# First conv unit of a hybrid decoder layer: one column chunk taken before its norm, two normalised meanwhile

## The chip, the cores and the metric

One core of one Trainium2 chip runs one layer of a decoder in float32. The metric is the device time in microseconds of the whole program. Engines: PE (TensorE, products), with PEld its weight loads; DVE (VectorE); ACT (ScalarE); POOL (GpSimd); SP, which only issues DMAs.

## The reference, cut to what matters

```
h = x * rsqrt(mean(x*x, over the 1024 channels) + eps) * g       # RMSNorm of 1040 positions
proj = h @ w_in                                                  # split among all branches
a, gate = u_conv                                                 # the conv branch's 2 x 1024 columns
y = a * sigmoid(gate)                                            # then a causal depthwise conv of 31 taps, ...
```

The other columns of proj are index queries and keys, attention q, k, v and merge gates; top-k attention, a merge product and a feed-forward part follow. rsqrt(mean) is one number for each position (a column here), so that it may be multiplied in before or after the product with w_in.

## The kernel before, in words

Channels lie on partitions, 8 tiles of 128 (k = 0 to 7); positions lie along the free dimension, 1044 with padding, cut into three chunks of 348 columns (c = 0, 1, 2). Every float32 product is made of three products of rounded parts: a value is split into a high part (a cast to fp32r) and a low part (value minus high part), and `mm` (L166 to L174, the matmul on L173) runs weight high x rows high, weight high x rows low, weight low x rows high, over the 8 tiles: 24 matmuls for one weight tile and one chunk.

`wload` (L114 to L127) loads a weight tile of 512 KB by SP (L117), casts its high part on ACT (L121) and makes the low part either on DVE (L123) or by an ACT negation (L125) and an accumulating DMA issued by POOL (L126). There are 2 raw buffers, 3 for high and 2 for low parts.

The start of the kernel: SP issues the first weight, x in 24 transfers (chunk by chunk, 8 tiles each, L210) with the second weight after the fourth of them (L212). WARM matmuls of the identity run on PE meanwhile (L222). Then, for each chunk in turn (L259 to L283): squares of the 8 tiles, six on ACT (L270) and two on DVE (L268); sums over partitions on PE, where a square is the stationary operand and a column of ones moves past it (L274: 3 blocks of 116 columns x 8 tiles, each recorded as 2 matmuls, so 48 records); the inverse root with one Newton step on [116, 3] tiles (`rstd_small`, L237 to L242: ACT's Sqrt is L238, the rest DVE); a broadcast over partitions by PE (L247, 6 records) into a PSUM bank; then per tile x times gain times that (L281, DVE), the cast to the high part `hh` (L282, ACT) and the low part `hl` (L283, DVE or POOL). The small sums and broadcasts use banks 6 and 7 in turn.

The first conv unit follows (L622 to L642): for each chunk 24 matmuls with the gate's weight into one bank triple and 24 with the value's into another; then tanh of half the gate on ACT (L631), (tanh + 1) times value on DVE (L641) into `g`, and the 31 taps of the depthwise conv (`conv_taps`, most of them on DVE, L554), which are dealt out as background work among the next units. Next come the index keys (L353, 72 matmuls, into the bank triple of the gate, so after the tanh has read it), four index-query units, merge gates, and conv units with other projections between them.

The order on each engine is fixed when the program is built: a planner takes instructions by priority and by its estimate of when their inputs are there (`urgent` raises the priority), and each engine then works its list in that order, waiting at semaphores. `tc.add_manual_dep` with NoSync is an order for the planner between two instructions of one engine, with no wait on the chip. Tiles of a full row of columns come from a pool of 31 (`ft`) or 4 (`tmp`) buffers.

## Time and profile before

| | us |
|---|---|
| median of 3 runs | 1860.74 (1859.44 to 1862.48) |
| profiled execution, its own time | 1865.77 |
| its span, first to last instruction | 1863.7 |
| busy: PE, DVE, ACT, POOL | 1790.6, 1231.9, 1049.3, 300.4 |
| mean granted PE clock | 0.975 of full speed |

The span is that of one profiled execution. Busy time of PE is from the start of a matmul to its modelled end, at whatever clock was granted: a busy PE at clock 0.5 does half the work. A row "[idle before <-releaser]" says how long the engine had waited and whose work ended the wait.

### The profile page before, as it was taken

The page shows a single profiled execution, that of the slowest core. Times are in us where ns is not written, and L with a number is a line of the kernel's source. Part 1 is how long each engine was busy: PE and PEld are TensorE (multiplying, and loading weights), DVE is VectorE, ACT ScalarE, POOL GpSimd, SP SyncE. Part 2 cuts the span into 40 slices and gives each one's busy share as a digit, 9 for nine tenths or more (in the row PEclk, how much of TensorE's full clock was granted, in tenths as well). Part 3 has the DMA queues.
Part 4 walks back from the last instruction along what each step waited for, and adds up shares of the span by engine and source line. Part 5 has one row for each costly group of instructions (what it writes and reads, how often), then busy time and mean ns, then how long its engine had stood idle before and what let it go on. Part 6 is the DMA issues. An engine that isn't in the chain of part 4 may idle for free. (4 is left out here: it accounts for less than half of the span.)

```text
span 1863.7 us, 29939 instructions
## 1 busy us (share of the span) xinstructions
PE 1790.6 (96%) x11956; PEld 1719.0 (92%) x11956; DVE 1231.9 (66%) x1949; ACT 1049.3 (56%) x1728; POOL 300.4 (16%) x310
## 2 busy tenths in 40 slices
PE   8989999999999999999999999899999999999987
PEld 7978899999999899899899999888999999999977
DVE  3598588997953472487843467845756575567677
ACT  3565587888999733488832246445434453444334
POOL 0243221111113122121100002011101100110002
PEclk7899999999999999999999999999999999999998
DMA  4434277776656488512246544365446634563432
GB/s 167 91 81 101 59 159 178 177 169 155 147 136 143 129 203 238 137 47 68 70 135 194 176 136 115 107 125 135 103 115 123 147 83 120 116 149 87 105 136 91
DMA packets 83899, 240.10 MB, mean 129 GB/s; under 512 B 8312, under 2 KB 28080, under 8 KB 83760
## 3 DMA queue, kind: packets, MB, share of 16 engines
q0 software_dynamic: 26208, 92.35, 27.9%
q1 hardware_dynamic: 57552, 145.84, 23.5%
q8 instruction: 93, 1.52, 0.3%
q14 instruction: 46, 0.38, 0.1%
HBM read 149.93 MB, written 65.09 MB: 115 GB/s over the span
## 5 line engine op out<-in xcount | busy, mean ns | idle before, releaser
L173 PE MATMUL PS<-hh,wh 128*128 128x342 f32 (+2 forms) x1096 | 196.0, 333 | 15.8 <-DVE qx0t L340 4.8
L1087 PE MATMUL PS<-B,ring 128*128 128x258 f32 (+1 forms) x1584 | 199.4, 286 | 5.5 <-DVE ub L1120 5.5
L1087 PEld LDWEIGHTS PS<-B,ring 128*128 128x128 f32 x1584 | 196.8, 193 | 8.2 <-DVE ub L1120 6.6
L173 PEld LDWEIGHTS PS<-hh,wh 128*128 128x128 f32 x1096 | 183.4, 195 | 20.2 <-DVE qx0t L340 5.2
L1155 PE MATMUL PS<-uh,ring 128*128 128x512 f32 (+2 forms) x736 | 188.6, 389 | 10.4 <-DVE x L1167 6.0
L459 ACT ACTIVATE junk<-sc,wn 128x1040 bf16<-128x1040 f32 (+6 forms) x217 | 182.3, 840 | 26.5 <-DVE wn L483 17.5
L173 PE MATMUL PS<-hh,wl 128*128 128x342 f32 (+2 forms) x1096 | 192.9, 328 | 0.8 <-DMA wl<-w_conv 0.8
L173 PE MATMUL PS<-hl,wh 128*128 128x342 f32 (+2 forms) x1096 | 191.1, 325 | 0.0
L1087 PE MATMUL PS<-h,ring 128*128 128x258 f32 (+1 forms) x1408 | 187.4, 282 | 3.7 <-ACT ring L1065 1.6
L173 PEld LDWEIGHTS PS<-hh,wl 128*128 128x128 f32 x1096 | 181.1, 192 | 2.7 <-DMA wl<-w_conv 1.1
L173 PEld LDWEIGHTS PS<-hl,wh 128*128 128x128 f32 x1096 | 179.4, 190 | 1.6
L1087 PEld LDWEIGHTS PS<-h,ring 128*128 128x128 f32 x1408 | 176.3, 189 | 4.4 <-ACT ring L1065 1.8
L1155 PEld LDWEIGHTS PS<-uh,ring 128*128 128x128 f32 x736 | 136.2, 190 | 39.7 <-issue 6.4
L121 ACT CAST wh<-wr 128x1024 fp32r<-128x1024 f32 x79 | 82.6, 1046 | 141.6 <-PE PS L173 69.5
L554 DVE SCALAR_TENSOR_TENSOR cb<-g,dwh,cb 128x1026 f32<-128x1026 f32 x105 | 138.0, 1316 | 34.8 <-DMA cb<-ct 34.7
L554 DVE SCALAR_TENSOR_TENSOR co<-g,dwh,co 128x1026 f32<-128x1026 f32 x113 | 152.2, 1350 | 1.4 <-ACT co L544 0.6
L1171 POOL DMA_DIRECT2D dx<-dn x72 | 62.4, 871 | 503.4 <-ACT dn L1170 498.0
L1065 ACT CAST ring<-ra 128x512 fp32r<-128x512 f32 x88 | 53.8, 620 | 126.3 <-PE PS L1087 64.6
L1066 DVE TENSOR_TENSOR ring<-ra,ring 128x512 fp32r<-128x512 f32 x88 | 60.0, 687 | 83.4 <-PE PS L1155 42.5
L1155 PE MATMUL PS<-ul,ring 128*128 128x512 f32 (+2 forms) x368 | 103.4, 390 | 0.0
L1087 PE MATMUL PS<-l,ring 128*128 128x258 f32 x704 | 100.1, 284 | 2.3 <-DMA l<-t 2.3
L1065 ACT CAST ring<-rb 128x512 fp32r<-128x512 f32 x66 | 41.0, 621 | 105.3 <-PE PS L1087 38.2
(438 smaller groups left out, 3552.8 us busy)
## 6 DMA issues: line engine op xcount, KB each, us to landing
dx<-dn POOLq DMA_DIRECT2D x72, 512.0 KB, 7.9
ra<-w_up SPq DMA_DIRECT2D x28, 512.0 KB, 3.8
rb<-w_up SPq DMA_DIRECT2D x22, 512.0 KB, 3.7
d<-w_down SPq DMA_DIRECT2D x22, 512.0 KB, 3.6
dth<-gt SPq DMA_DIRECT2D x16, 513.0 KB, 8.0
gate<-dth SPq DMA_DIRECT2D x16, 513.0 KB, 4.2
wr<-w_conv SPq DMA_DIRECT2D x16, 512.0 KB, 4.2
wr<-w_gate SPq DMA_DIRECT2D x16, 512.0 KB, 4.1
```

The lines of the kernel that those rows point to most:

```text
L121: act.copy(wh[:, :nk * P], raw[:, :nk * P])
L173: pe.matmul(ps[:, ci, :n], lhsT=ww[:, sl], rhs=rr[k][:, c0:c0 + n], start=(k == 0 and pi == 0), stop=(k == nk - 1 and pi == 2))
L459: act.activation(junk[:, :n], sc[j][:, PAD:PAD + n], AF.Sign, bias=bits.bitcast(F32)[:, slot[j]:slot[j] + 1], accum_out=cnt[:, slot[j]:slo ...
L554: dve.scalar_tensor_tensor(a, g[:, w:w + LQ], wt[w], a, op0=ALU.mult, op1=ALU.add)
L1065: hi = act.copy(t[:, w0], raw)
L1066: dve.tensor_tensor(t[:, w1], raw, f(t)[:, w0], op=ALU.subtract)
L1087: pe.matmul(ps[:, b, p0:p0 + nn], lhsT=t[:, o + k * P:o + (k + 1) * P], rhs=B[rows][k][e][:, r0:r0 + nn], start=(pi == 0 and k == 0), stop ...
L1155: pe.matmul(ps[:, c, :w], lhsT=t[:, wo:wo + P], rhs=rows[k][x][:, c0 + c * w:c0 + (c + 1) * w], start=(pi == 0 and k == 0), stop=(pi == 2 ...
L1171: pool.dma_start(d_x2[m], t[:, :SEQ], accum_op=ALU.add)
```

## The change

Seven things are altered, all in the start of the kernel, the first conv unit and the index keys.

1. Chunk 0 is taken raw: `raw_columns` makes `hh` and `hl` of x times gain, without 1/rms (ACT's scaled copy, DVE's scaled subtraction), and the first unit's 48 matmuls on chunk 0 use these. What comes out of them is multiplied by 1/rms afterwards: the gate's chunk 0 by a DVE multiply into `th` (the other two are copied there by ACT, and the tanh works on `th` in SBUF), the value's through one more DVE multiply on the first 348 columns of `g`.
2. Chunks are normalised in the order 1, 2, 0. 1/rms goes into an SBUF tile `rms` (ACT copy) instead of being read from PSUM. Chunk 0's rows are normalised last, for the index keys and everything behind them.
3. All 8 squares of a chunk are on ACT; those of tiles 4 to 7 are added to those of tiles 0 to 3 on DVE, so that PE sums four tiles and not eight (24 records a chunk).
4. Low parts: of chunks 1 and 0 all on DVE, after all the scalings of the chunk; of chunk 2 by an ACT negation and 8 accumulating DMAs that POOL issues. No subtraction is left on POOL.
5. In the first unit's chunks 1 and 2 and in the index keys the order of the three parts is high x high, weight low x rows high, weight high x rows low (`rows_last`); the index keys take the chunks in the order 1, 2, 0.
6. The second weight is loaded after all of chunk 0's x; the third weight's low part (the index keys') is made on DVE.
7. Orders for the planner (`behind`): chunk 1's squares after the raw casts; chunk 2's squares of tiles 0 to 3 after those, of tiles 4 to 7 after chunk 1's root; chunk 2's adds after chunk 1's Newton step; the next weight cast after chunk 2's rms copy.

```diff
@@ -86,6 +86,13 @@
     def f(t):
         return t.bitcast(F32)
 
+    def behind(a, b):
+
+        tc.add_manual_dep(a.ins, b.ins.name,
+                          mybir.DependencyInfo(mybir.DependencyClass.NoSync, mybir.DependencyReason.DATA), reason="order")
+
+    behind_act = [None]
+
     def urgent():
         return tc.high_priority(offset=600)
 
@@ -118,8 +125,11 @@
         wh = base.tile([P, KT * P], F32R, tag="wh", bufs=3, name=f"wh{i}")
         wl = base.tile([P, KT * P], F32R, tag="wl", bufs=2, name=f"wl{i}")
         with urgent():
-            act.copy(wh[:, :nk * P], raw[:, :nk * P])
-            if i < 2 or i >= ix_mg[0][0]:
+            e = act.copy(wh[:, :nk * P], raw[:, :nk * P])
+            if behind_act[0]:
+                behind(e, behind_act[0])
+                behind_act[0] = None
+            if i < 3 or i >= ix_mg[0][0]:
                 placed[0] = dve.tensor_tensor(wl[:, :nk * P], raw[:, :nk * P], f(wh)[:, :nk * P], op=ALU.subtract)
             else:
                 act.activation(wl[:, :nk * P], raw[:, :nk * P], AF.Copy, scale=-1.0)
@@ -163,10 +173,11 @@
     ix_mg = [[wadd(w_merge[m], KT) for m in range(KT)] for _ in range(2)]
     NPAIR = DFF // P
 
-    def mm(ps, w, rh, rl, nk, cols, woff=0):
+    def mm(ps, w, rh, rl, nk, cols, woff=0, rows_last=False):
 
         wh, wl = w
-        for pi, (ww, rr) in enumerate(((wh, rh), (wh, rl), (wl, rh))):
+        parts = ((wh, rh), (wl, rh), (wh, rl)) if rows_last else ((wh, rh), (wh, rl), (wl, rh))
+        for pi, (ww, rr) in enumerate(parts):
             for k in range(nk):
                 sl = slice(woff + k * P, woff + (k + 1) * P)
                 for ci, (c0, n) in enumerate(cols):
@@ -208,9 +219,8 @@
     for c in range(NCH):
         for k in range(KT):
             nc.sync.dma_start(xs[k][:, c * CW:(c + 1) * CW], xT[:, k, c * CW:(c + 1) * CW])
-            if c == 0 and k == KT // 2 - 1:
-                wload(1)
         if c == 0:
+            wload(1)
             nc.sync.dma_start(vec[:, V_DW:], vecs[:, V_DW:])
     ident = base.tile([P, P], F32, name="ident")
     make_identity(nc, ident)
@@ -229,23 +239,26 @@
         for b in range(nb):
             pe.matmul(dst[:w, b:b + 1], lhsT=src[:, c0 + b * w:c0 + (b + 1) * w], rhs=ones, start=True, stop=True)
 
+    root, newton = [None], [None]
+
     def rstd_small(src, w, n, name):
 
         v = base.tile([P, 9], F32, tag="stv", bufs=2, name=name + "v")[:w, :n]
         r = base.tile([P, 9], F32, tag="str", bufs=2, name=name + "r")[:w, :n]
         t = base.tile([P, 9], F32, tag="stt", bufs=2, name=name + "t")[:w, :n]
         dve.tensor_scalar(v, src[:w, :n], 1.0 / D, EPS, op0=ALU.mult, op1=ALU.add)
-        act.activation(t, v, AF.Sqrt)
+        root[0] = act.activation(t, v, AF.Sqrt)
         dve.reciprocal(r, t)
         dve.tensor_tensor(t, r, v, op=ALU.mult)
         dve.scalar_tensor_tensor(t, t, -0.5, r, op0=ALU.mult, op1=ALU.mult)
-        dve.scalar_tensor_tensor(r, t, 1.5, r, op0=ALU.add, op1=ALU.mult)
+        newton[0] = dve.scalar_tensor_tensor(r, t, 1.5, r, op0=ALU.add, op1=ALU.mult)
         return r
 
     def bcast_mm(dst, small, w, b0, nb):
         for b in range(nb):
             pe.matmul(dst[:, b * w:(b + 1) * w], lhsT=small[:, b0 + b:b0 + b + 1].to_broadcast([w, P]),
                       rhs=ident[:w, :w], start=True, stop=True)
+
 
 
     sc_pool = tc.tile_pool(name="sc", bufs=1)
@@ -255,32 +268,72 @@
     act.activation(warm, warm, AF.Sqrt)
     hh = [ft(f"hh{k}", F32R) for k in range(KT)]
     hl = [ft(f"hl{k}", F32R) for k in range(KT)]
+    rms = ft("rms")
     BW = CW // 3
-    for c in range(NCH):
+    first_ps = (psm(), psm())
+    tail, done = [None], [None]
+
+    def raw_columns(c):
+        cs = slice(c * CW, (c + 1) * CW)
+        for k in range(KT):
+            tail[0] = act.activation(hh[k][:, cs], xs[k][:, cs], AF.Copy, scale=vcol(V_MG + k))
+            dve.scalar_tensor_tensor(hl[k][:, cs], xs[k][:, cs], vcol(V_MG + k), f(hh[k])[:, cs], op0=ALU.mult,
+                                     op1=ALU.subtract)
+
+    def first_products(c):
+        for ps, w in zip(first_ps, units[0][2]):
+            mm(ps[:, c:c + 1, :], wdone[w], hh, hl, KT, LCOLS[c:c + 1], rows_last=c > 0)
+
+    def column_rms(c):
         cs = slice(c * CW, (c + 1) * CW)
         sqs = []
         for k in range(KT):
             if k % 3 == 0:
-                sqt = ft(f"sq{c}_{k}")
+                sqt = (tmp if c == 2 else ft)(f"sq{c}_{k}")
             sq = sqt[:, (k % 3) * CW:(k % 3 + 1) * CW]
             sqs.append(sq)
-            if k % 4 == 3:
-                dve.tensor_tensor(sq, xs[k][:, cs], xs[k][:, cs], op=ALU.mult)
-            else:
-                act.activation(sq, xs[k][:, cs], AF.Square)
+            e = act.activation(sq, xs[k][:, cs], AF.Square)
+            if c == 2 and k >= 4:
+                behind(e, root[0])
+            elif c:
+                behind(e, tail[0])
+                tail[0] = e
+            if k >= 4:
+                e = dve.tensor_tensor(sqs[k % 4], sqs[k % 4], sq, op=ALU.add)
+                if c == 2:
+                    behind(e, newton[0])
         sb = bank("s", (6, 7))
         for b in range(3):
-            for k in range(KT):
-                pe.matmul(sb[:BW, b:b + 1], lhsT=sqs[k][:, b * BW:(b + 1) * BW], rhs=ones, start=(k == 0),
-                          stop=(k == KT - 1))
+            for e in range(4):
+                pe.matmul(sb[:BW, b:b + 1], lhsT=sqs[e][:, b * BW:(b + 1) * BW], rhs=ones, start=(e == 0), stop=(e == 3))
         r = rstd_small(sb, BW, 3, f"n1{c}")
         sb = bank("s", (6, 7))
         bcast_mm(sb, r, BW, 0, 3)
+        done[0] = act.copy(rms[:, cs], sb[:, :CW])
+
+    def norm_columns(c):
+        cs = slice(c * CW, (c + 1) * CW)
         for k in range(KT):
             x = xs[k][:, cs]
-            dve.scalar_tensor_tensor(x, x, vcol(V_MG + k), sb[:, :CW], op0=ALU.mult, op1=ALU.mult)
+            dve.scalar_tensor_tensor(x, x, vcol(V_MG + k), rms[:, cs], op0=ALU.mult, op1=ALU.mult)
             act.copy(hh[k][:, cs], x)
-            (pool if k % 3 == 2 else dve).tensor_tensor(hl[k][:, cs], x, f(hh[k])[:, cs], op=ALU.subtract)
+        for k in range(KT):
+            if c == 2:
+                act.activation(hl[k][:, cs], f(hh[k])[:, cs], AF.Copy, scale=-1.0)
+                pool.dma_start(hl[k][:, cs], xs[k][:, cs], accum_op=ALU.add)
+            else:
+                dve.tensor_tensor(hl[k][:, cs], xs[k][:, cs], f(hh[k])[:, cs], op=ALU.subtract)
+
+    raw_columns(0)
+    first_products(0)
+    for c in (1, 2, 0):
+        with urgent():
+            column_rms(c)
+        norm_columns(c)
+        if c:
+            first_products(c)
+        if c == 2:
+            behind_act[0] = done[0]
     del xs
 
     def rope_table(name, src):
@@ -353,7 +406,8 @@
     def index_keys(w):
 
         ps = psm()
-        mm(ps, wget(w), hh, hl, KT, LCOLS)
+        for c in (1, 2, 0):
+            mm(ps[:, c:c + 1, :], wget(w), hh, hl, KT, LCOLS[c:c + 1], rows_last=True)
         kx, sw, wt = tmp("kxt"), tmp("kxs"), tmp("kxw")
         kh_, kl_ = kx_hl[:] = [ft("kxh", F32R), ft("kxl", F32R)]
         with urgent():
@@ -618,28 +672,32 @@
     GOFF = CONVW - 1 - Q0
     for kind, i, w in units:
         if kind == "conv":
-            ps = PS[:, 0:3, :] if i == 1 else psm()
+            if i:
+                ps = PS[:, 0:3, :] if i == 1 else psm()
+            th = tmp(f"th{i}")
             if i == 0:
-                wg, wa, psa = wget(w[0]), wget(w[1]), psm()
-                for c in range(NCH):
-                    mm(ps[:, c:c + 1, :], wg, hh, hl, KT, LCOLS[c:c + 1])
-                    mm(psa[:, c:c + 1, :], wa, hh, hl, KT, LCOLS[c:c + 1])
+                wget(w[1])
+                ps, pa = first_ps
+                with urgent():
+                    act.copy(c3(th[:, CW:LC], CW), ps[:, 1:, :CW])
+                    dve.tensor_tensor(th[:, :CW], ps[:, 0, :CW], rms[:, :CW], op=ALU.mult)
+                    act.activation(th[:, :LC], th[:, :LC], AF.Tanh, scale=0.5)
+                background(8, 1)
             else:
                 mm(ps, wget(w[0]), hh, hl, KT, LCOLS)
-            th = tmp(f"th{i}")
-            with urgent():
-                act.activation(c3(th[:, :LC], CW), ps[:, :, :CW], AF.Tanh, scale=0.5)
-            background(8, 1)
-            if i == 0:
-                ps = psa
-            else:
-                ps = PS[:, 0:3, :] if i == 1 else psm()
-                mm(ps, wget(w[1]), hh, hl, KT, LCOLS)
+                with urgent():
+                    act.activation(c3(th[:, :LC], CW), ps[:, :, :CW], AF.Tanh, scale=0.5)
+                background(8, 1)
+                pa = PS[:, 0:3, :] if i == 1 else psm()
+                mm(pa, wget(w[1]), hh, hl, KT, LCOLS)
             g = ft(f"g{i}")
             pool.memset(g[:, 0:GOFF], 0.0)
             with urgent():
-                dve.scalar_tensor_tensor(c3(g[:, GOFF:GOFF + LC], CW), c3(th[:, :LC], CW), 1.0, ps[:, :, :CW],
+                dve.scalar_tensor_tensor(c3(g[:, GOFF:GOFF + LC], CW), c3(th[:, :LC], CW), 1.0, pa[:, :, :CW],
                                          op0=ALU.add, op1=ALU.mult)
+                if i == 0:
+                    dve.tensor_tensor(g[:, GOFF:GOFF + CW], g[:, GOFF:GOFF + CW], rms[:, :CW], op=ALU.mult)
+                    del rms
             tasks.append(conv_taps(i, g))
             if i == KT - 1:
                 tasks.append(layer_norm())
@@ -1065,9 +1123,7 @@
             hi = act.copy(t[:, w0], raw)
             dve.tensor_tensor(t[:, w1], raw, f(t)[:, w0], op=ALU.subtract)
         if j < RB:
-            tc.add_manual_dep(hi.ins, placed[0].ins.name,
-                              mybir.DependencyInfo(mybir.DependencyClass.NoSync, mybir.DependencyReason.DATA),
-                              reason="room")
+            behind(hi, placed[0])
 
     def block(i, n):
 
```

## Rows read from the trace of the kernel before

**Rows 1.** Page, busy time, share of the span and instructions of each engine.
```profile
PE 1790.6 (96%) x11956; PEld 1719.0 (92%) x11956; DVE 1231.9 (66%) x1949; ACT 1049.3 (56%) x1728; POOL 300.4 (16%) x310
```

**Rows 2.** Busy time by stretch: from:to us, length, each engine, PE clock, DMA.
```profile
0.00:12.00 12.00, 8.59 (x56) 8.25 (x57) 3.51 (x5) 5.90 (x10) 2.41 (x31) 1.00 0.84 291
...
12.00:28.00 16.00, 10.42 (x47) 10.06 (x47) 9.00 (x20) 6.05 (x15) 1.89 (x2) 0.51 0.66 235
...
36.00:56.00 20.00, 20.00 (x91) 20.00 (x92) 8.71 (x24) 4.27 (x10) 1.97 (x3) 0.51 0.08 28
...
56.00:72.00 16.00, 14.05 (x88) 13.76 (x87) 7.08 (x14) 8.25 (x13) 2.92 (x3) 0.98 0.08 27
...
92.00:152.00 60.00, 51.08 (x244) 46.11 (x243) 59.81 (x52) 33.85 (x44) 26.14 (x14) 0.92 0.37 79
...
232.00:592.00 360.00, 356.78 (x2256) 355.52 (x2257) 291.78 (x407) 315.64 (x548) 66.65 (x72) 1.00 0.68 158
```

**Rows 3.** Timeline, 0 to 85 us: start, us taken, engine, line, operation, [idle before].
```profile
5.77 1.26 ACT L270 ACTIVATE sq<-x 128x348 f32<-128x348 f32 x3
...
16.47 0.16 DVE L237 TENSOR_SCALAR n10v<-PS 116x3 f32<-116x3 f32 x1 [5.35 <-PE PS L274]
...
17.72 1.63 PE L247 MATMUL PS<-ident,n10r 116*128 116x116 f32 x6 [1.29 <-DVE n10r L242]
...
22.16 1.04 ACT L121 CAST wh<-wr 128x1024 fp32r<-128x1024 f32 x1 [5.29 <-DMA wr<-w_idx]
...
23.64 4.72 PE L173 MATMUL PS<-hh,wh 128*128 128x348 f32 x15 [4.29 <-ACT hh L282]
...
26.18 4.71 ACT L270 ACTIVATE sq<-x 128x348 f32<-128x348 f32 x12
...
32.36 4.97 PE L274 MATMUL PS<-ones,sq 128*116 128x1 f32 x44
...
42.92 1.61 PE L247 MATMUL PS<-ident,n11r 116*128 116x116 f32 x6
...
44.32 7.37 PE L274 MATMUL PS<-ones,sq 128*116 128x1 f32 x38
...
44.56 3.99 DVE L281 SCALAR_TENSOR_TENSOR x<-x,vec,PS 128x348 f32<-128x348 f32 x8 [6.00 <-PE PS L247]
...
48.47 3.15 DVE L283 TENSOR_TENSOR hl<-x,hh 128x348 fp32r<-128x348 f32 x6
...
51.55 4.70 PE L173 MATMUL PS<-hh,wh 128*128 128x348 f32 x15
...
58.42 0.82 PE L247 MATMUL PS<-ident,n12r 116*128 116x116 f32 x6
...
72.12 4.08 PE L173 MATMUL PS<-hh,wh 128*128 128x348 f32 x24 [2.07 <-ACT th L631]
```

**Rows 4.** Groups of instructions by shape, 0 to 75 us: busy us, mean ns.
```profile
L274 PE MATMUL PS<-ones,sq 128*116 128x1 f32 x144 | 22.2, 283 | 1.9 <-ACT sq L270 1.7 <-DVE sq L268 0.2
...
L268 DVE TENSOR_TENSOR sq<-x 128x348 f32<-128x348 f32 x6 | 2.8, 510 | 0.0
...
L123 DVE TENSOR_TENSOR wl<-wr,wh 128x1024 fp32r<-128x1024 f32 x2 | 2.5, 1226 | 7.6 <-ACT wh L121 7.6
...
L631 ACT ACTIVATE th<-PS 128x1044 f32<-128x1044 f32 x1 | 1.0, 1041 | 0.0
```

**Rows 5.** Groups by shape on ACT, 1700 us to the end: a scaled copy.
```profile
L1211 ACT ACTIVATE x<-x,vec 128x256 f32<-128x256 f32 x8 | 3.9, 498 | 0.0
```

**Rows 6.** POOL's timeline near 1149 us: start, us taken, two DMA issues.
```profile
1149.17 1.75 POOL L982 DMA_DIRECT2D l<-t  x2 [0.69 <-ACT l L981]
```

**Rows 7.** Line L982's accumulating DMAs, 257 KB each, by source line.
```profile
DMA to landing us min/median/max: 3.4/5.2/6.8
```

**Rows 8.** PE's waits, 92 to 152 us: total, times, longest.
```profile
PE PS L173 <- DVE qx0t L340: 4.8, 1, 4.8
```

**Rows 9.** DVE's timeline, 92 to 152 us: one conv tap.
```profile
107.26 1.27 DVE L554 SCALAR_TENSOR_TENSOR co<-g,dwh,co 128x1026 f32<-128x1026 f32 x1
```

## The prediction

> **What bounds the kernel now.** I read the page's busy line first: PE is busy 96% of the span [rows 1], so the end moves only with PE's work, PE's clock, or PE's idle time. Then I took the busy time by stage [rows 2]. From 232 to 592 us PE is busy 356.8 of 360 us at clock 1.00: nothing to win or lose there except by a shift of the whole. The first 72 us are different. PE is busy in most of it, but the granted clock is 0.51 from 12 to 28 and from 36 to 56 us, half of full speed, that is 1.2 instead of 2.4 GHz. Last I read that stage in order of time [rows 3]. Its product work is one conv unit: 2 weights x 3 chunks x 24 = 144 products, which at the rate after 72 us (24 in 4.08, 0.17 us each) is 24.5 us. It takes until 70 us, because each chunk repeats one chain: squares, 48 one-column sums on PE, five small DVE steps and a root, six broadcasts, eight scalings on DVE, eight casts on ACT, and only then products. The first product starts at 23.64; the chunk-1 chain is through at 51.55, having waited in PE's own queue: its broadcast (42.92 us) and the 38 sums of chunk 2 (7.37 us) stand ahead of its products. At 72.12 the index keys begin. From there PE's work is the same before and after the change, so I forecast one number: when the index keys begin after it.
>
> **The change part by part.**
>
> *Chunk 0 raw.* Its products no longer wait for any statistic. They need x, which was squared from 5.77 us, and a scaled cast on ACT. One costs between 0.39 (twelve squares in 4.71) and 0.50 us (the scaled copies at the end, though of fewer elements) [rows 3, 5]; I take 0.45, since the width of the first and the scale of the second both apply: 8 x 0.45 from 5.9 to 9.5. The low parts on DVE, 8 x 0.53 (six in 3.15) after the weight's 1.23 [rows 3, 4], end near 11.5. The second weight now lies behind four more x transfers (0.7 MB, at the 291 GB/s of the first 12 us 2.4 us [rows 2]); its low part is ready near 13. That is covered by the 24 products of the first weight. The 48 products take 48 x 0.17 = 8.2 us at the high clock and 48 x 0.31 (15 in 4.70) = 15 at the low one, from about 7.5. They end between 16 and 23.
>
> *Chunk 1.* Squares 8 x 0.39 as x lands, to about 14.5; four DVE adds of 0.53, the last at 15.2; half the sums, 24 instead of 48, at 0.11 (44 in 4.97) or 0.19 (38 in 7.37): 2.7 or 4.6 us. Root and small steps 1.25 (16.47 to 17.72), broadcast 0.82 or 1.63, a copy to SBUF of 0.4, scaling (eight in 3.99) and cast 0.9 [rows 3]. First chunk-1 product at 21.5 to 24.5, as chunk 0's end: no gap worth counting. This is the large term: that point was 51.55. DVE then owes 4.0 of scaling, 4.2 of low parts and 2.1 of chunk 2's adds; the last low part comes near 33, the chunk's 48 products end near 34 (37 at the low clock).
>
> *Chunk 2.* Its rms is ready near 30, but DVE is free only near 33: scaling to 37, casts to 37.5, eight negations on ACT (0.39) to 40.6. Then POOL issues eight accumulating DMAs. The trace has no such transfer of 174 KB; the nearest are of 257 KB: two issues in 1.75, so 0.88 each, and 3.4 to 6.8 us to land, median 5.2 [rows 6, 7]. I take the median: last issue starts near 44.5, last low part near 50, the last products 0.5 later. The 32 products on the high parts are long done (39 to 43), so here PE waits for POOL's queue. Behind these eight on that queue stands only the third weight's transfer, needed 12 us into the index keys.
>
> *Halved sums* are inside the above: 72 of 144 records go, 72 x (22.2/144 = 0.154) = 11.1 us of PE [rows 4]; twelve DVE adds (6.4 us) come for six DVE squares (2.8) [rows 4].
>
> *After the unit.* Index keys reuse the gate's banks: ACT must copy two of them, 0.8 of the 1.04 that the tanh took [rows 4], so they begin near 51.5. If the clock dropped in PE's wait for chunk 2, their first 5 us run at half rate: 2.5 more. I take 54. Their third weight's low part comes from DVE (1.23) under the first 8 products; chunk 0's scaling and low parts, 8.2 us of DVE, lie under the 48 products on chunks 1 and 2 (8.2 us), and its squares earlier in ACT's gaps. The order put on the next cast (behind the rms copy) removes a stall like that of 22.16, where ACT sat 5.29 us for a weight's DMA with chunk 0's casts queued behind. Conv unit 0's g gains two DVE multiplies of 0.53 and its tanh now follows a copy: about 3 us later against the index keys. In 92 to 152 DVE is busy 59.8 of 60 and PE 51.1 [rows 2], so some of that comes back as PE waits: between 0 and 3 us, I take 0.5.
>
> *Sum.* 72.1 - 54 = 18 saved, less 0.5: 17.5. Ends: at the high clock, with landings in 3.4 us and the wait filled, the index keys start at 45 (27 saved); with the low clock throughout, 144 x 0.31 + 72 x 0.19 + 3 x 1.63 = 63 us from 7.5, so 70.5 (1.5 saved). The profiled run is 1865.77 (span 1863.7 and 2.1 around it); the sum gives 1848.3. The median shown, 1860.74, lies 5.0 under the profiled run: 1843.
>
> *The clock.* Rows first: from 36 to 56 us PE is busy 20.00 of 20 and the grant is 0.51; ahead of its fall at 36 PE ran one-column sums, and it is 0.98 over 56 to 72, after wide products from 51.55 [rows 2, 3]. The Trainium skill, page "TensorE: Matmul & The Clock Gate", Part 1, says that the engine is throttled by default and that being busy releases it. By that rule PE, fed from 7.5 on, would run high to the end of chunk 1 and the index keys would begin 2 to 3 us earlier than I take; by the rows a busy PE can stay low for 20 us. The rows decide, and the sum above leaves the chunk-0 clock open.
>
> **The rivals.**
> 1. *All works.* The clock stays at 1.00 and POOL's transfers land early. For it: sums halve and lie among wide products. Against it: the median landing is 5.2. Start 44 to 47: 25 to 28 saved, 1833 to 1836.
> 2. *DVE and POOL become the stage's bound.* DVE's work in it grows from about 30 to 38 us: raw low parts 4.2, adds 6.4, scalings 12, low parts 8.4, weights 3.7, small steps 3. If chunk 0's share runs ahead of chunk 2's scaling (8 us), or PE's queue holds the second weight's products behind low parts that land late and runs them at 0.31, the index keys start at 62 to 67: 5 to 10 saved, 1851 to 1856.
> 3. *Slower: conv taps get ahead.* PE's and DVE's orders are fixed beforehand from estimated times, and a new start gives a new order. DVE's taps of unit 0 take about 1.2 us each, and PE already waits 4.8 for one rope multiply behind them [rows 8, 9]. If the index-query multiplies each fall behind four or five more taps, four times, PE waits 16 to 24 us more. It decides from 15 more taps on (18 us): about 1866. Against it: taps and rope multiplies alternate nearly one to one, and nothing in that code is changed.
> 4. *No change.* The index keys do start early but chunk 0's normalised rows come so late (past 78 us) that their end stays. It would need 25 us of other DVE work ahead of them, which I don't find: 1858 to 1863.
>
> **How the numbers follow.** Forecast 1843 (1837 to 1849, 12 to 24 saved): 0.62. Rival 1: 0.13. Rival 2: 0.13. Rival 3: 0.07. Rival 4: 0.05. What can be told from no change here is 0.2%, 3.7 us. Faster by more: 0.62 + 0.13 + 0.13 = 0.88; within: 0.05; slower: 0.07. The range runs over rival 1's bound and rival 2's: 1832 to 1857, leaving out rivals 3 and 4 and a little below, some 0.15.
>
> **What would show it.** Right: a first wide product before 8 us; chunk 1's first between 21 and 25; one-column sums of 24 records per chunk; PE waiting for a DMA on the low parts near 40 to 50; index keys near 54; afterwards every stage shifted by the same. Wrong: clock 0.5 through the index keys; chunk 2's high parts behind chunk 0's scaling on DVE; the saving visible at the index keys but smaller at 232 us, which would be rival 3.

## The result, and the profile after

1843.91 us median (1840.62 to 1850.65, 6 runs) against 1861.58 for the kernel before in the same session. The ratio, taken over all runs and so not quite the quotient of the two medians, is 0.9912, 95% interval 0.9891 to 0.9933. The forecast was 1843. The execution that was profiled took 1850.64 us (span 1848.9), near the top of its runs; its span is 14.8 us under that of before.

Page, busy time, as [rows 1]: PE has 12 us less, the other three a little more.

```profile
PE 1778.6 (96%) x11884; PEld 1704.3 (92%) x11884; DVE 1239.5 (67%) x1964; ACT 1060.2 (57%) x1753; POOL 303.0 (16%) x311
```

Busy time by stretch, as [rows 2]. The clock of 36 to 56 us is 0.93 where it was 0.51. From 92 to 152 PE is busy even less than before, 49.94 of 60, and from 232 on it is as busy as it was (356.36 of 360, 356.78 before).

```profile
12.00:28.00 16.00, 14.71 (x88) 14.63 (x86) 8.11 (x20) 9.93 (x26) 0.11 (x1) 0.72 0.77 270
36.00:56.00 20.00, 18.73 (x115) 17.48 (x115) 13.46 (x30) 14.94 (x31) 8.11 (x9) 0.93 0.68 122
...
92.00:152.00 60.00, 49.94 (x258) 46.50 (x257) 55.61 (x56) 32.35 (x48) 22.56 (x14) 0.89 0.39 87
232.00:592.00 360.00, 356.36 (x2249) 354.93 (x2249) 289.58 (x402) 314.46 (x544) 72.12 (x72) 1.00 0.67 155
```

PE in order of time, as [rows 3], cut (L184 products, L308 one-column sums, L259 broadcasts): the raw products start at 6.99 and not at 23.64. Chunk 1's products (29.52) stand behind both its own sums and those of chunk 2. The index keys' first full run of products is at 53.13, not 72.12: 19.0 us earlier.

```profile
6.99 2.50 PE L184 MATMUL PS<-hh,wh 128*128 128x348 f32 x7
11.60 2.12 PE L184 MATMUL PS<-hh,wh 128*128 128x348 f32 x8 [2.12 <-ACT wh L128]
...
20.20 2.10 PE L308 MATMUL PS<-ones,sq 128*116 128x1 f32 x20
23.58 1.63 PE L259 MATMUL PS<-ident,n11r 116*128 116x116 f32 x6 [1.29 <-DVE n11r L254]
25.00 4.66 PE L308 MATMUL PS<-ones,sq 128*116 128x1 f32 x24
29.52 4.09 PE L184 MATMUL PS<-hh,wh 128*128 128x348 f32 x15
...
36.95 0.91 PE L259 MATMUL PS<-ident,n12r 116*128 116x116 f32 x6
...
51.88 0.58 PE L184 MATMUL PS<-hl,wh 128*128 128x348 f32 x2 [0.57 <-DMA hl<-x]
...
53.13 2.60 PE L184 MATMUL PS<-hh,wh 128*128 128x348 f32 x8 [0.36 <-ACT th L682]
```

ACT and then DVE behind the first unit: after PE's last product of it ACT copies two chunks of the gate (52.34), then serves a weight cast and two casts of rows, loads a table, and only at 56.10 comes the tanh. `g` is made at 57.21, 4.1 us after the index keys began (in the kernel before both were at 72.1). The first conv tap starts at 69.08, since it waits 9.76 us for a DMA. ACT, then DVE:

```profile
52.34 0.74 ACT L682 COPY th<-PS 128x696 f32<-128x696 f32 x1 [1.81 <-PE PS L184]
52.98 1.05 ACT L128 CAST wh<-wr 128x1024 fp32r<-128x1024 f32 x1
53.92 0.87 ACT L319 CAST hh<-x 128x348 fp32r<-128x348 f32 x2
54.81 1.28 ACT L684 ACT_TABLE_LOAD   x1
56.10 1.08 ACT L684 ACTIVATE th<-th 128x1044 f32<-128x1044 f32 x1
```

```profile
57.21 1.24 DVE L696 SCALAR_TENSOR_TENSOR g<-th,PS 128x1044 f32<-128x1044 f32 x1 [1.82 <-ACT th L684]
...
69.08 4.58 DVE L608 SCALAR_TENSOR_TENSOR cb<-g,dwh,cb 128x1026 f32<-128x1026 f32 x2 [9.76 <-DMA cb<-ct]
...
96.23 1.28 DVE L608 SCALAR_TENSOR_TENSOR co<-g,dwh,co 128x1026 f32<-128x1026 f32 x1
97.42 3.11 DVE L608 SCALAR_TENSOR_TENSOR cb<-g,dwh,cb 128x1026 f32<-128x1026 f32 x1
100.45 1.08 DVE L393 TENSOR_TENSOR qx1t<-PS,c 128x896 f32<-128x896 f32 x1
```

The same in the kernel before, ACT and DVE together; the first tap waited for that DMA there too, 10.64 us:

```profile
69.73 1.28 ACT L631 ACT_TABLE_LOAD   x1
71.03 1.04 ACT L631 ACTIVATE th<-PS 128x1044 f32<-128x1044 f32 x1
...
72.10 1.24 DVE L641 SCALAR_TENSOR_TENSOR g<-th,PS 128x1044 f32<-128x1044 f32 x1 [5.74 <-ACT th L631]
...
83.98 2.61 DVE L554 SCALAR_TENSOR_TENSOR cb<-g,dwh,cb 128x1026 f32<-128x1026 f32 x2 [10.64 <-DMA cb<-ct]
```

PE's waits from 92 to 240 us, as [rows 8]: the rope multiply of index query 1 stands behind a tap (97.42 above), and PE waits 5.9 us for it. The third row is new: a conv weight's low part, 2.4 us (0.8 in the kernel before).

```profile
PE PS L184 <- DVE qx1t L393: 5.9, 1, 5.9
PE PS L458 <- DVE r L467: 2.8, 1, 2.8
PE PS L184 <- DMA wl<-w_conv: 2.4, 1, 2.4
```

The tap at 97.42 takes 3.11 us, the one ahead of it 1.28. A multiply runs on POOL at that time:

```profile
97.17 2.27 POOL L447 TENSOR_TENSOR qs<-qx0t,qs 64x896 fp32r<-64x896 f32 x1 [4.15 <-ACT qs L446]
```

Of unit 0's 27 taps on DVE twenty take 1.27 to 1.29 us here, and the seven that take 2.15 to 3.26 all lie beside such an operation of POOL, 12 us more in all. POOL is the likely cause; no run took its operations away.

Landmarks tell where the 19 us went. The first merge gate's tanh came at 157.45 before and 138.34 after (19.1 earlier), the third one's at 309.36 and 294.12 (15.2 earlier), the last computing instruction 15.2 earlier. So 4 us were lost between the first and the third gate, and on balance none behind them. Before, then after:

```profile
157.45 1.01 ACT L665 ACTIVATE gt<-PS 128x1026 f32<-128x1026 f32 x1
...
309.36 1.00 ACT L665 ACTIVATE gt<-PS 128x1026 f32<-128x1026 f32 x1
```

```profile
138.34 1.01 ACT L723 ACTIVATE gt<-PS 128x1026 f32<-128x1026 f32 x1
...
294.12 1.00 ACT L723 ACTIVATE gt<-PS 128x1026 f32<-128x1026 f32 x1
```

### The profile page after: what moved, and what is told of

The parts are those of the page before. It is cut to its first block, busy times and chain, and to the rows that moved or that the text cites. A ratio compares the mean times of both kernels' runs of the same rounds, so it can differ in the third digit from the quotient of the medians.

```text
span 1848.9 us, 29862 instructions
## 1 busy us (share of the span) xinstructions
PE 1778.6 (96%) x11884; PEld 1704.3 (92%) x11884; DVE 1239.5 (67%) x1964; ACT 1060.2 (57%) x1753; POOL 303.0 (16%) x311
## 5 line engine op out<-in xcount | busy, mean ns | idle before, releaser
L184 PE MATMUL PS<-hh,wh 128*128 128x342 f32 (+2 forms) x1096 | 199.1, 333 | 14.7 <-DVE qx1t L393 5.9
L184 PEld LDWEIGHTS PS<-hh,wh 128*128 128x128 f32 x1096 | 183.6, 195 | 20.3 <-DVE qx1t L393 6.3
L184 PE MATMUL PS<-hh,wl 128*128 128x342 f32 (+2 forms) x1096 | 191.4, 326 | 2.4 <-DMA wl<-w_conv 2.4
L184 PE MATMUL PS<-hl,wh 128*128 128x342 f32 (+2 forms) x1096 | 192.6, 326 | 0.9 <-DMA hl<-x 0.9
L184 PEld LDWEIGHTS PS<-hh,wl 128*128 128x128 f32 x1096 | 179.9, 191 | 4.3 <-DMA wl<-w_conv 2.7
L184 PEld LDWEIGHTS PS<-hl,wh 128*128 128x128 f32 x1096 | 179.3, 190 | 3.3 <-DMA hl<-x 1.7
L608 DVE SCALAR_TENSOR_TENSOR cb<-g,dwh,cb 128x1026 f32<-128x1026 f32 x105 | 143.3, 1368 | 36.4 <-DMA cb<-ct 32.6
```

What stands on the lines that cost most here:

```text
L184: pe.matmul(ps[:, ci, :n], lhsT=ww[:, sl], rhs=rr[k][:, c0:c0 + n], start=(k == 0 and pi == 0), stop=(k == nk - 1 and pi == 2))
L608: dve.scalar_tensor_tensor(a, g[:, w:w + LQ], wt[w], a, op0=ALU.mult, op1=ALU.add)
```

## The experiments

Twelve kernels; each batch has its own runs of the kernel before (medians 1863.18 for experiments 1 to 4, 1860.85 for 5 to 8, 1864.93 for 9, 11 and 12, 1861.61 for 10). One table serves all. From the profiled execution, in us: "keys" is the index keys' first full run of products, "tap" the first DVE tap, "gate 1" and "gate 3" the tanh of those merge gates, "3-1" the time between them, "wait" PE's wait for a conv weight's low part in that time, "profiled" the execution's own time. "Median" and "ratio" (to the kernel before on the same chip, with its 95% interval) are over all runs. "Late shared taps" is the edit of experiment 5; "kernel 5" is the kernel of experiment 5.

```
   kernel                           keys   tap  gate 1 gate 3  3-1   wait profiled  median   ratio
   before                           72.1  84.0  157.5  309.4  151.9  0.8  1865.77
 2 halved sums alone                68.2  80.2  153.8  305.1  151.2  0.7  1862.08  1855.64  0.9963 (0.9951-0.9976)
 6 before, late shared taps         68.8  71.4  141.8  299.0  157.2  2.1  1850.27  1854.55  0.9962 (0.9947-0.9977)
 4 after, full sums                 64.4  77.1  145.2  302.6  157.4  3.7  1858.23  1855.69  0.9963 (0.9949-0.9976)
 3 after, no raw chunk              64.7  74.8  143.8  294.5  150.8  0.7  1849.35  1849.05  0.9936 (0.9914-0.9958)
 7  the same, late shared taps      62.1  65.1  137.6  293.6  156.0  2.1  1849.58  1852.34  0.9957 (0.9945-0.9969)
   after                            53.1  69.1  138.3  294.1  155.8  2.4  1850.64  1843.91  0.9912 (0.9891-0.9933)
 1 after again                      55.4  71.1  140.7  295.0  154.3  1.3  1850.96  1851.21  0.9933 (0.9910-0.9955)
 5 after, late shared taps          53.2  60.8  133.6  284.6  151.0  0.8  1841.85  1842.15  0.9907 (0.9894-0.9920)
11  the same, chunk 2 low on DVE    50.4  63.2  140.0  296.5  156.5  3.1  1855.15  1851.44  0.9931 (0.9915-0.9946)
12  the same, chunk 2's root first  58.4  66.1  139.0  289.7  150.7  0.7  1846.61  1847.53  0.9908 (0.9890-0.9926)
 8 after, weight 10's low on DVE    50.3  65.3  133.7  289.2  155.5  3.0  1850.46  1848.93  0.9942 (0.9929-0.9955)
 9 after, weight 11's low on DVE    54.3  69.0  137.6  294.0  156.5  2.9  1848.69  1852.68  0.9937 (0.9919-0.9956)
10 after, weight 12's low on DVE    50.9  65.6  134.2  285.5  151.3  none 1845.95  1845.68  0.9923 (0.9904-0.9943)
```

**1. The changed kernel again**, without an edit.

> The changed kernel once more, for a second profile. Mine (what is gained is gained before the index keys, all later differences are the order's): index keys begin at 53.1 +- 0.3 us again, and the 4.7 us that the first profile gives back between 174 and 230 us (a 2.4 us wait for a weight's low part at 201, then clock 0.64) are there again or, if the run is near 1842, smaller. Rival (the loss lies elsewhere, in the tail): the tanh of conv unit 1 stands at the same place in both profiles and the runs differ after 592 us. Time 1840 to 1851.

1851.21 (1841.65 to 1854.87). The two ratios, 0.9912 and 0.9933, have overlapping intervals, but one kernel spreads over 0.8%: a difference of 3 us between two kernels hardly shows in the totals.

The index keys began at 55.44, 2.3 us later and not within the 0.3 that was expected; the wait for the weight is there again, at 1.3 us. The order of work on every engine is the same in both executions, and up to 150 us also in kernels 8 to 10. So those five show what an execution does by itself: keys at 50.3 to 55.4, first tap at 65.3 to 71.1, gate 1 at 133.7 to 140.7. The time from the keys to gate 1 varies less, 83.3 to 85.3. One landmark against one other tells little under 5 us; a stretch between two landmarks tells more.

**2. The kernel before with halved sums, nothing else.**

```diff
+            if k >= 4:
+                dve.tensor_tensor(sqs[k % 4], sqs[k % 4], sq, op=ALU.add)
...
-            for k in range(KT):
+            for e in range(4):
...
```

> The kernel before with one part of the change: squares of tiles 4 to 7 added to those of 0 to 3 on DVE, PE sums four tiles. Mine: 72 records go from PE, but the chain through PE's queue stays; of 11 us some 5 to 9 are gained at the index keys (72.1 to 63 to 67), 1852 to 1856. Rival (the sums are the gain): 11 us or more, index keys at 61 or earlier, 1850 or less.

Ratio 0.9963, a total in the expected range. In the profiled execution, the slowest of its ten, the index keys come 4.0 us earlier, short of the 5 to 9 expected, and every later landmark by 3 to 4. These 4.0 do not stand clear of the spread: kernel 6, whose order is that of the kernel before up to its first tap, began its index keys 3.3 us earlier.

**3. The changed kernel, with all three chunks normalised (0, 1, 2), none raw.**

```diff
-    raw_columns(0)
-    first_products(0)
-    for c in (1, 2, 0):
+    for c in (0, 1, 2):
...
```

The rest of the edit goes with it: the tanh reads PSUM, nothing is multiplied by 1/rms afterwards, and the index keys take the chunks as 0, 1, 2.

> The changed kernel with chunk 0 normalised first like the others (order 0, 1, 2, tanh straight from PSUM, no multiply by 1/rms afterwards), everything else of the change kept. Mine: PE's first product moves from 7 to about 20 us and the index keys begin at 62 to 66, so 9 to 13 us of the gain go: 1852 to 1857. Rival (sums and orders are the gain, raw columns matter little because PE is not what ends the stage): index keys at 53 to 57, 1843 to 1848.

The index keys begin at 64.65, 11.5 us later than in the changed kernel, as expected. The total does not follow: 1849.05, under the 1852 to 1857 expected, and 0.9936 beside 0.9933 for the changed kernel in the same batch. The head start of 11.5 us is 5.7 at the first tap, 5.4 at the first gate, 0.4 at the third (5 us go between these gates, where this kernel waits 0.7 us for the weight and not 2.4; see experiment 10). DVE's timeline shows the first loss: here `g` follows the index keys' start at once, where the changed kernel needs 4.1 us more for its copy, table load and tanh; and here too the first tap waits 8.9 us for the DMA.

```profile
64.63 1.24 DVE L692 SCALAR_TENSOR_TENSOR g<-th,PS 128x1044 f32<-128x1044 f32 x1 [8.98 <-ACT th L680]
74.75 2.61 DVE L606 SCALAR_TENSOR_TENSOR cb<-g,dwh,cb 128x1026 f32<-128x1026 f32 x2 [8.87 <-DMA cb<-ct]
```

**4. The changed kernel, PE summing all eight tiles** (raw chunk kept).

```diff
-                e = dve.tensor_tensor(sqs[k % 4], sqs[k % 4], sq, op=ALU.add)
...
-            for e in range(4):
...
+            for k in range(KT):
...
```

> The changed kernel with PE summing all 8 squares again (48 records a chunk, no adds on DVE). Mine: chunk 1's sums stand before its products and cost 24 records more, 2.6 to 4.6 us, chunk 2's as much, partly hidden under the wait for POOL: index keys at 56 to 60, 1847 to 1852. Rival (the sums are the gain): 11 us back, index keys at 64, 1854 or more.

The index keys begin at 64.42, where the rival had them (64; 56 to 60 was expected): undoing the halved sums costs as much there as undoing the raw chunk, 11 us. The clock from 12 to 16 us is 0.57 in both executions compared, so that they start alike. The granted clock is 0.50 to 0.54 in six of the seven 4-us stretches from 24 to 52 us. The total is 1855.69 (0.9963), above the 1847 to 1852 expected.

After these four my theory was: once the index keys run, DVE and not PE sets the pace (it is busy 7.9 us or more of every 8 from 72 to 136 us), and its work begins with the first tap, so what counts is the first tap. The taps wait because two shared taps (made by ACT, added to both accumulators by DMAs) come first in the chain.

**5. The changed kernel, the shared taps of conv unit 0 issued after DVE's 27.**

```diff
+        if i:
+            shared_taps()
         for w in range(2, CONVW - shared):
...
+        if i == 0:
+            shared_taps()
```

> The changed kernel, with the two shared taps of conv unit 0 (made by ScalarE, added by a DMA) issued after VectorE's 27 taps instead of ahead of them, so that VectorE's first tap no longer waits 9.8 us for that DMA. Theory (from about 69 to 136 us VectorE is full with the taps and the rope multiplies, and the time follows its first tap, not the index keys' first product): index keys stay at 53 to 55, the first tap moves from 69.1 to about 61, TensorE's wait for the rope multiply of index query 1 (5.9 us) falls under 2, the first gate's tanh (138.3) comes 5 to 8 us earlier and the whole is 4 to 8 us under the changed kernel's 1844 to 1851, ratio to before 0.987 to 0.991. Rival (the time follows TensorE's order from the index keys on; VectorE only fills gaps): first tap at 61, the tanh within 1 us of 138, ratio 0.992 to 0.994 as for the changed kernel.

The first tap moves 8.3 us, with the index keys at 53.2 as in the changed kernel (clock from 12 to 16 us 0.58 and 0.57); the first gate comes 4.7 us earlier, just short of the 5 to 8 expected, and the third 9.5, of which 4.8 arise between the gates, where the wait for the weight is 0.8 us. From the keys to gate 1 it takes 80.4 us, outside the 83.3 to 85.3 of the five equal executions. 1842.15 (1841.36 to 1844.05): in the expected direction, though the interval overlaps both of the changed kernel's. The tap waits no longer for a DMA, but for ACT's first product:

```profile
60.77 1.29 DVE L611 SCALAR_TENSOR_TENSOR co<-g,dwh,co 128x1026 f32<-128x1026 f32 x1 [1.37 <-ACT co L598]
```

PE's waits from 92 to 240 us. The wait for index query 1 is halved, and query 2 has one of its own: 5.1 together, where 5.9 was expected to fall under 2.

```profile
PE PS L184 <- DVE qx1t L393: 2.7, 1, 2.7
PE PS L184 <- DVE qx2t L393: 2.4, 1, 2.4
...
PE PS L184 <- DMA wl<-w_conv: 0.8, 1, 0.8
```

**6. The same edit on the kernel before**, none of the change in it.

> The kernel before, with the same one edit of the shared taps and nothing of the change. Theory (VectorE's first tap sets it): index keys stay at 72.1, first tap moves from 84.0 to about 75, the first gate's tanh (157.5) 5 to 8 us earlier, total 1853 to 1857, ratio 0.995 to 0.997: the edit gives without any earlier products what the changed kernel only gets by 19 us of earlier products in part. Rival (TensorE's order from the index keys on sets it): within 1 us of before.

0.9962: 6 us, as expected. The index keys began 3.3 us earlier in this execution, which the edit does not touch; the first gate comes 15.6 us earlier, where 5 to 8 were expected. From 92 to 152 us PE's waits fall to these two rows, and its clock is 1.00 there instead of 0.92:

```profile
PE PS L173 <- DVE qx1t L340: 3.1, 1, 3.1
PE PS L173 <- ACT gt L670: 0.5, 1, 0.5
```

```profile
92.00:152.00 60.00, 56.31 (x307) 52.72 (x306) 52.23 (x50) 42.98 (x57) 30.43 (x19) 1.00 0.59 132
```

**7. No raw chunk (as 3), with the late shared taps.**

> Chunk 0 normalised first (as in the run before without raw products) together with the late shared taps. Theory (first tap sets it): first tap moves from 74.8 to about 67.5, total 3 to 7 us under the 1849 of the same kernel without the edit, ratio 0.990 to 0.992, and 3 to 7 us above the changed kernel with the late taps, since its gate came 7 us later: with the DMA wait gone the raw chunk is worth something at the end. Rival (a later stage evens all out, whatever comes first): equal to the changed kernel with the late taps within 2 us.

Half a miss. Against kernel 5 it is 10 us slower, intervals apart. Not all of this is the raw chunk: 4.0 us stand at the first gate, and 5.0 more arise before the third, where this kernel waits for the weight and kernel 5 hardly does. And it is not faster than kernel 3 (0.9957 beside 0.9936): the 6 us won up to the first gate are lost before the third, where PE waits 2.1 us for a conv weight. The table's column 3-1 has two levels: 151 to 152 us where that wait is 0.8 or none, 154 to 157 where it is 1.3 to 3.7.

**8 to 10. That weight.** Its low part is made by ACT and an accumulating DMA. I made it on DVE instead, and took the wrong weight twice.

```diff
-            if i < 3 or i >= ix_mg[0][0]:
+            if i < 3 or i == 12 or i >= ix_mg[0][0]:
```

> The changed kernel, with the low part of conv unit 1's second weight made on VectorE as for the first weights instead of on ScalarE and a DMA; TensorE waited 2.4 us for it at 203.4 and then ran 16 products at 0.64 of the clock. Theory (about 4 us of the gain are given back at this place): the wait goes, the landmark of conv unit 2 keeps the 19 us that conv unit 1 has instead of 15, total 2 to 4 us under the changed kernel. Rival (the order after it evens this out, or VectorE's 1.2 us lands in its full stretch): within 1.5 us of the changed kernel.

> The changed kernel, with the low part of conv unit 2's first weight (index 11) made on VectorE; the earlier try of this kind moved the weight before it, and the wait of 3.0 us stayed. Theory (about 4 to 5 us of the gain are lost between the first gate's tanh and the third one, where this weight's low part lands 2.4 us late and the clock then stands at 0.64): the stretch from the first gate's tanh to the third shrinks from 155.8 us to 151, as in the kernels in which that wait was 0.8 us or less, and the total falls 3 to 5 us under the changed kernel run beside the others (1844 to 1851). Rival (the loss lies in the order after it): 155 to 157 stays, total within 1.5 us.

> The changed kernel, with the low part of conv unit 2's second weight (index 12) made on VectorE; the two earlier tries of this kind (indices 10 and 11) moved other weights, and the wait stayed at 3.0 and 2.9 us. In TensorE's order it is the products of index 12 that stand directly ahead of the wait at 203. Theory (some 5 us of the gain are lost there, 2.4 as the wait and the rest as a clock of 0.64): the wait falls under 0.5 us, the stretch from the first gate's tanh to the third shrinks from 155.8 us to 151 to 153, total 3 to 5 us under the changed kernel (ratio 0.989 to 0.991). Rival (a wait that goes here comes back later, so that the place is not a cost of its own): the wait goes and 155 to 156 stays, total within 1.5 us of the changed kernel's two measurements.

With 10 and 11 the wait stayed (3.0 and 2.9 us) and 3-1 stayed at 155.5 and 156.5. With 12, conv unit 2's second weight, the wait is gone and 3-1 is 151.3. So the 4 us come from this wait; the two levels of column 3-1 say the same. The place, in the changed kernel: behind the wait the clock falls to 0.64, that is, to the low level for most of these 4 us.

```profile
203.38 4.37 PE L184 MATMUL PS<-hh,wl 128*128 128x348 f32 x16 [2.38 <-DMA wl<-w_conv]
```

```profile
204.00:208.00 4.00, 4.00 (x20) 4.00 (x19) 0.00 (x0) 0.00 (x0) 0.00 (x1) 0.64 0.00 0
```

With weight 12 on DVE the same products run from 195.04 on, and PE is busy throughout at 1.00:

```profile
195.00:199.00 4.00, 4.00 (x25) 3.81 (x24) 3.45 (x6) 1.20 (x2) 0.59 (x1) 1.00 0.20 83
```

The total, 1845.68 at a ratio of 0.9923 (0.9904 to 0.9943), is short of the 0.989 to 0.991 expected, and its interval holds both of the changed kernel's ratios: the stage is settled, the end only likely.

**11. Kernel 5, with chunk 2's low parts on DVE** instead of POOL's eight DMAs.

```diff
-            if c == 2:
-                act.activation(hl[k][:, cs], f(hh[k])[:, cs], AF.Copy, scale=-1.0)
-                pool.dma_start(hl[k][:, cs], xs[k][:, cs], accum_op=ALU.add)
...
```

> The changed kernel with the late shared taps (1842.15), and with chunk 2's low parts made by VectorE instead of ScalarE and eight accumulating DMAs on POOL's queue. Theory (the DMAs, issued 40.8 to 48.0, make the last products of conv unit 0 wait only 0.3 to 1.0 us, but the gate's th and the clock follow them; VectorE's eight take 8 times 0.52 in idle time): index keys 1 to 3 us earlier, first tap 1 to 3 us earlier, total 0 to 3 us less. Rival (POOL's queue sets the end of conv unit 0, as the prediction had it at 50 us): index keys 4 us or more earlier.

A miss: the ratio is 0.9931 where kernel 5 had 0.9907. The index keys come 2.8 us earlier, within the 1 to 3 expected, but this cannot be put down to the edit: the clock from 12 to 16 us was 1.00 in this execution (0.58 in kernel 5), and kernels 8 and 10, whose clock was 1.00 there too, began their keys at 50.3 and 50.9 without it. DVE now does chunk 0's eight low parts between the two multiplies of `g`, so the first tap is 2.4 us later, and the weight's wait is back at 3.1.

```profile
56.09 1.24 DVE L697 SCALAR_TENSOR_TENSOR g<-th,PS 128x1044 f32<-128x1044 f32 x1
57.24 3.54 DVE L321 TENSOR_TENSOR hl<-x,hh 128x348 fp32r<-128x348 f32 x8
60.69 0.52 DVE L700 TENSOR_TENSOR g<-g,rms 128x348 f32<-128x348 f32 x1
```

**12. Kernel 5, chunk 2's root steps and scaling ahead of chunk 1's low parts and chunk 0's adds.**

```diff
-                if c == 2:
-                    behind(e, newton[0])
+                if c != 1:
+                    behind(e, newton[0] if c else scaled[0])
...
+                if c == 1:
+                    behind(e, scaled[0])
...
```

> The changed kernel with the late shared taps (1842.15), and with chunk 2's root steps and scaling put ahead of chunk 1's low parts and chunk 0's square adds in VectorE's and ScalarE's order. Theory (chunk 2's broadcast ratios came at 37.9 instead of 30 because its root steps stood behind that work on VectorE, though its sums were done at 29.5): chunk 2's ratios 32 to 34, its products' end and the index keys 2 to 4 us earlier, total 1 to 4 us less. Rival (TensorE, fully busy from 29.5 on with the products of chunk 1, sets it): index keys within 1 us of 53 to 55, or later, since chunk 1's low parts now come later.

The theory missed. Chunk 2's broadcast moves from 36.99 in kernel 5 only to 35.21; chunk 1's low parts now come later, PE waits, its clock is 0.50 from 40 to 52 us, and the index keys begin at 58.35, 5 us later. In the traces these 5 us are carried on: the first tap comes 5.3 us later than in kernel 5, gate 1 5.4, gate 3 5.0, and the profiled execution takes 4.8 us longer. The ratio, 0.9908 beside 0.9907, does not show it; the two were taken on different chips (medians of the kernel before 1864.93 and 1860.85), and each interval reaches some 2.5 to 3.5 us to either side.

## Why the prediction was right

**The number and the sum.** 17.5 us were forecast; the medians differ by 17.7, the profiled spans by 14.8. In the traces the sum is 19.0 saved at the index keys and 3.8 given back, where 18 and 0.5 stood. That the median comes within 1 us of the forecast is luck: the same kernel's second set of runs lies 12.0 us under its kernel before, at the edge of the 12 to 24 that were forecast.

**Index keys at 54:** measured 53.13 and 55.44. Five executions of this order of work spread from 50.3 to 55.4. The steps inside were less right. The raw products start at 6.99 (7.5 forecast) and end near 20.3 (16 to 23 forecast). Chunk 1's first product is at 29.52, not at 21.5 to 24.5: its sums waited in PE's queue for the last raw products, and chunk 2's 24 sums, 4.66 us at the low clock, stand ahead of it there, which I did not count. For the same reason, and because DVE took chunk 0's adds and chunk 1's low parts before chunk 2's small steps, chunk 2's 1/rms was ready at 37.9 and not near 30. POOL began to issue at 40.8; the eight DMAs landed in 3.1 to 5.7 us, median 4.1 (5.2 taken), and PE waited for them for 0.9 us in all. The late middle was made good by the clock: once products ran, it was 1.00 in each 4-us stretch from 36 to 52 us, so that chunk 1's products and most of chunk 2's lay under chunk 2's chain.

**The clock.** PE is busy throughout 24 to 32 us at a clock of 0.50, first with sums, then with products; over 32 to 36 us it is 0.90:

```profile
24.00:28.00 4.00, 4.00 (x23) 4.00 (x22) 3.52 (x8) 3.02 (x9) 0.00 (x0) 0.50 0.18 71
28.00:32.00 4.00, 4.00 (x18) 4.00 (x19) 4.00 (x10) 3.82 (x10) 0.00 (x0) 0.50 0.01 2
32.00:36.00 4.00, 4.00 (x27) 4.00 (x26) 3.56 (x12) 0.20 (x1) 0.00 (x0) 0.90 0.00 0
```

It had fallen between 22 and 23 us (0.77, then 0.50), behind chunk 1's one-column sums and as PE began to wait 1.29 us for the small steps; it rose between 32 and 33 us, in the wide products that began at 29.52. Before the change it fell at 36, while such sums ran. Sums alone do not always lower it: chunk 0's, from 35.60 to 38.78, ran at 1.00. The rule that the prediction took from the Trainium skill, page "TensorE: Matmul & The Clock Gate", Part 1 (throttled by default, being busy releases it), is not what these rows show: PE is busy 8.00 of 8 us from 24 to 32 at 0.50, as it was 20.00 of 20 at 0.51 before the change.

**Halved sums** were put at 11.1 us of PE. At the index keys they are 11.3 (64.42 against 53.13) beside a raw chunk. Alone they are 4.0 in one execution, not clear of the spread; that other waits take over there is likely, not shown.

**The step that failed** is "From there PE's work is the same before and after the change, so I forecast one number: when the index keys begin". PE's work is the same, but its waits are not, and the index keys' start does not order what follows: keys at 50.4, 58.4 and 64.7 us go with a third gate at 296.5, 289.7 and 294.5 (kernels 11, 12 and 3). From the keys to gate 1 the traces take between 73.0 (kernel 6) and 89.6 us (kernel 11). Two things stand between. First, DVE's stretch begins with the first tap, which gained 14.9 us and not 19. I had put the tanh 3 us later against the index keys and the give-back at 0.5: the delay is 4.1, of which 1.28 is a table load ahead of the tanh. In the kernel before the load stood there too (69.73), but the index keys waited for the tanh; kernel 3 has it at 57.19, before its products are done, and the tanh at 63.56 waits for PE alone. (The Trainium skill, page "ScalarE: Activation LUTs", section "What ACT_TABLE_LOAD costs", gives about 1283 ns for the load, as the row has it, and about 1380 ns for a drain; no row here shows the drain, the tanh starts 0.01 us behind the load.) From the index keys to the first gate's tanh it is 85.3 us before and 85.2 after, so that 0.5 looks right; but kernel 3 does it in 79.1, which is how a head start of 11.5 us became 5.4. Second, in the new order PE comes to weight 12 before its low part has landed, for 4 us; no step of the prediction had that.

**The rivals.** Rival 1 (all works) fell with chunk 1. Rival 2 named the right engine at the wrong place: DVE is the bound behind the index keys, not ahead of them. Rival 3's sign, a saving that is smaller at 232 us than at the index keys, did show, though not by its mechanism: the loss was a weight, not a tap. Rival 4 is out.

**What stays open.** Why DVE's stretch from the first tap to the first gate takes 68 to 70 us in some orders and 72 to 77 in others; the planner's order on DVE differs between them, and no run changed that order alone. The long taps beside POOL are not the answer by their number: seven in the changed kernel, five in kernel 5, which takes 3.5 us more. From the third gate's tanh to their end the profiled executions take 1549.5 (kernel 6) to 1559.5 us (kernel 8), 1554.8 in the changed kernel; no run shows why, and it hides gains of a few us from the totals. And no version here is clearly faster than the changed kernel: kernel 5 has the lowest ratio, but its interval overlaps.

## What to carry to other kernels

Ask of each landmark you forecast who else must pass it: the time of PE's next work is worth what the next full engine's first instruction gains, so follow the head start to that instruction. Where a DMA adds into an accumulator ahead of a long chain of an engine that is full, put it behind the chain. When an edit changes the estimates of a planner, look for waits that are new far behind the edit before you call the gain lost or kept. And profile one kernel several times before you read a shift of a landmark between two kernels.

## What the runs showed of the hardware that was not expected

The level of the clock in the first products differs between executions with the same order of work up to there. From 12 to 16 us it was 0.57 in the changed kernel and 1.00 in the kernel with weight 12 on DVE, whose order differs only from 190 us on; the index keys then began 2.2 us earlier. PE's first products ahead of that stretch began at 6.99 and 7.54 us, and PE then waited 2.12 and 2.36 us for the second weight's cast. In the five equal executions a clock of 1.00, 1.00, 0.57, 0.67 and 0.50 there goes with index keys at 50.3, 50.9, 53.1, 54.3 and 55.4 (kernels 8, 10, the changed kernel, 9 and 1). Changed kernel, then kernel 10:

```profile
12.00:16.00 4.00, 4.00 (x18) 4.00 (x17) 3.20 (x6) 3.97 (x10) 0.00 (x0) 0.57 1.06 366
```

```profile
12.00:16.00 4.00, 4.00 (x26) 4.00 (x26) 3.20 (x6) 4.00 (x10) 0.00 (x0) 1.00 1.05 343
```
